# A row softmax on one core: tiles of twelve rows in four buffers instead of eight rows in six, with six of eleven stores moved to Pool's queue

## Chip, cores, metric

One core of a Trainium2 chip. The metric is the device time of one execution in microseconds (us), of which the span in a profile leaves out about 2. The kernel before takes 317.6 us.

## The reference

```python
"x": np.random.randn(32, 512, 1024).astype(np.float32), "temperature": 0.5
scaled = x / temperature
shifted = scaled - np.max(scaled, axis=-1, keepdims=True)
exp_x = np.exp(shifted)
return (exp_x / np.sum(exp_x, axis=-1, keepdims=True)).astype(np.float32)
```

There are 16,384 rows of 1,024 float32, so 128 rows of the matrix for each of the 128 partitions. 67.1 MB are read and 67.1 MB written.

## The kernel before

A tile holds `ROWS` consecutive matrix rows in each partition, so that each partition's part of a transfer is one contiguous piece (8 rows x 4 KB = 32 KB). It is loaded by SP, changed in place, and stored; its buffer then goes to a later load. A pass is a group of a tile's rows that goes through one maximum; `PASSES` lists the passes of each tile. VectorE (DVE) takes the maximum and divides by the sum, ScalarE (ACT) does the exponential with its sum. The code is abridged.

```python
ROWS = 8; BUFS = 6
PASSES = [[4, 4]] * 2 + [[8]] * 12 + [[4, 4]] * 2
WHOLE = (2, 4, 6, 8, 10, 12)     # tiles divided by one instruction
ALONE = 14
...
def maximum(g):
    nc.vector.tensor_reduce(out=top, in_=tiles[i][:, a:a+k, :], axis=X, op=extreme)
    nc.vector.tensor_scalar_mul(bias, in0=top, scalar1=-scale)
def exponential(g):
    for b in range(k):
        nc.scalar.activation(row, row, Exp, bias=bias[:, b:b+1], scale=scale, accum_out=sums[:, b:b+1])
def divide(g):
    nc.vector.reciprocal(recip, sums)
    if i in WHOLE: nc.vector.tensor_mul(xt, xt, recip.unsqueeze(2).to_broadcast([P, k, d]))
    else:          # row by row: tensor_scalar_mul
def store(g):      # g == 0: one row by Pool's queue; else, when the tile is done, by ACT's
    nc.scalar.dma_start(out=dram(of, i)[:, a:, :], in_=tiles[i][:, a:, :])
    load()         # the next tile, by SP's queue, when this store has landed
...
for g in range(len(groups) + 1):   # cut: the last tiles divide before the next maximum
    maximum(g); exponential(g); divide(g - 1); store(g - 1)
```

## Time and profile before

| | before |
|---|---|
| time, median | 317.61 us (317.17 to 317.79, 6 runs) |
| span of the profile | 315.7 us |
| DVE, ACT, Pool busy | 251.0, 148.1, 1.3 us |
| DMA, share of 16 engines | 99.0% |
| rate with loads and stores running | 433 GB/s |

On the page, a digit of the DMA row is the busy share of one fortieth of the span in tenths. q1 is SP's queue of loads, q10 ACT's queue, q0 Pool's. The lines themselves stand in the prediction.

### The profile page before, as it was taken

The page shows a single profiled execution, that of the slowest core. Times are in us where ns is not written, and L with a number is a line of the kernel's source. Part 1 is how long each engine was busy: PE and PEld are TensorE (multiplying, and loading weights), DVE is VectorE, ACT ScalarE, POOL GpSimd, SP SyncE. Part 2 cuts the span into 40 slices and gives each one's busy share as a digit, 9 for nine tenths or more (in the row PEclk, how much of TensorE's full clock was granted, in tenths as well). Part 3 has the DMA queues.
Part 4 walks back from the last instruction along what each step waited for, and adds up shares of the span by engine and source line. Part 5 has one row for each costly group of instructions (what it writes and reads, how often), then busy time and mean ns, then how long its engine had stood idle before and what let it go on. Part 6 is the DMA issues. An engine that isn't in the chain of part 4 may idle for free. (4 is left out here: it accounts for less than half of the span.)

```text
span 315.7 us, 534 instructions
## 1 busy us (share of the span) xinstructions
DVE 251.0 (79%) x146; ACT 148.1 (47%) x257; POOL 1.3 (0%) x5
## 2 busy tenths in 40 slices
DVE  0399999999679795897949979399793999979710
ACT  0176637680906519074290833808247091564700
POOL 0001000000000000000000000000000000000000
DMA  8999999999999999999999999999999999999996
GB/s 328 415 448 421 369 441 434 465 400 461 404 457 407 457 411 457 428 436 436 428 448 415 448 415 449 411 465 403 461 403 461 403 461 403 461 403 461 407 457 274
DMA packets 4755, 134.24 MB, mean 425 GB/s; under 512 B 528, under 2 KB 528, under 8 KB 656
## 3 DMA queue, kind: packets, MB, share of 16 engines
q1 hardware_dynamic: 2304, 67.11, 49.7%
q10 hardware_dynamic: 2304, 66.59, 48.9%
q0 software_dynamic: 144, 0.52, 0.4%
q14 instruction: 3, 0.02, 0.0%
HBM read 67.11 MB, written 67.11 MB: 425 GB/s over the span
## 5 line engine op out<-in xcount | busy, mean ns | idle before, releaser
L77 ACT ACTIVATE xt<-xt,bias 128x1024 f32<-128x1024 f32 x128 | 145.2, 1135 | 136.6 <-DVE bias L71 127.1
L68 DVE TENSOR_REDUCE top<-xt 128x8 f32<-128x8192 f32 (+1 forms) x20 | 139.5, 6976 | 44.4 <-DMA xt<-in_x_dram 44.4
L95 DVE TENSOR_SCALAR xt<-xt,recip 128x1024 f32<-128x1024 f32 x80 | 54.3, 748 | 0.5
L92 DVE TENSOR_TENSOR xt<-xt,recip 128x8192 f32<-128x8192 f32 x6 | 52.2, 8692 | 0.2
L77 ACT ACTIVATION_READ_ACCUMULATOR xt<-xt,bias 128x1 f32 x128 | 23.9, 187 | 0.0
L77 ACT ACT_TABLE_LOAD x1 | 1.3, 1283 | 13.3 <-DMA xt<-in_x_dram 13.3
L89 DVE RECIPROCAL recip<-sums 128x8 f32<-128x8 f32 (+1 forms) x20 | 3.8, 188 | 4.1 <-ACT xt L77 4.1
L71 DVE TENSOR_SCALAR bias<-top 128x8 f32<-128x8 f32 (+1 forms) x20 | 3.4, 171 | 0.7
L104 POOL DMA_DIRECT2D out_dram<-xt x1 | 1.1, 1142 | 23.4 <-DVE xt L95 23.4
L143 POOL MEMSET const-bfloat16-1.0<- 128x1 bf16 x1 | 0.1, 96 | 0.0
L143 POOL MEMSET const-float32-0.0<- 128x1 f32 x1 | 0.1, 93 | 0.2 <-issue 0.2
L143 POOL MEMSET const-float32-1.0<- 128x1 f32 x1 | 0.1, 93 | 0.0
L143 POOL MEMSET const-uint8-127<- 128x1 uint8 x1 | 0.1, 93 | 0.0
## 6 DMA issues: line engine op xcount, KB each, us to landing
xt<-in_x_dram SPq DMA_DIRECT2D x16, 4096.0 KB, 51.2
out_dram<-xt ACTq DMA_DIRECT2D x15, 4096.0 KB, 28.0
out_dram<-xt ACTq DMA_DIRECT2D x1, 3584.0 KB, 23.2
out_dram<-xt POOLq DMA_DIRECT2D x1, 512.0 KB, 19.6
```

The source lines that it names most:

```text
L68: nc.vector.tensor_reduce(out=top, in_=tiles[i][:, a : a + k, :], axis=mybir.AxisListType.X, op=extreme)
L71: nc.vector.tensor_scalar_mul(bias, in0=top, scalar1=-scale)
L77: nc.scalar.activation(tiles[i][:, a + b, :], tiles[i][:, a + b, :], mybir.ActivationFunctionType.Exp, bias=bias[:, b : b + 1], scale=scal ...
L89: nc.vector.reciprocal(recip, sums)
L92: nc.vector.tensor_mul(xt, xt, recip.unsqueeze(2).to_broadcast([P, k, d]))
L95: nc.vector.tensor_scalar_mul(tiles[i][:, a + b, :], in0=tiles[i][:, a + b, :], scalar1=recip[:, b : b + 1])
L104: nc.gpsimd.dma_start(out=dram(of, i)[:, :1, :], in_=tiles[i][:, :1, :])
L143: nc = _bacc.Bacc("TRN2", target_bir_lowering=False, num_devices=1)
```

## The change

The intent: larger pieces per partition (48 KB) at the same memory, passes of six rows, five of eleven tiles divided whole, and the first six stores taken out of ACT's instruction stream. The tiny copy ahead of the first store is there to hold it until the third load has landed. The diff is abridged.

```diff
-ROWS = 8
-BUFS = 6
+PASSES = [[4, 4, 4]] + [[6, 6]] * 9 + [[4, 4]]
+BUFS = 4
-PASSES = [[4, 4]] * 2 + [[8]] * 12 + [[4, 4]] * 2
-WHOLE = (2, 4, 6, 8, 10, 12)
+WHOLE = (2, 3, 4, 6, 8)
+BY_POOL = 6
-ALONE = 14
+ALONE = 9
 ...                       # cut: ROWS becomes rows[i] = sum(PASSES[i]) throughout
 def store(g):
-        if g == 0:
-            nc.gpsimd.dma_start(out=dram(of, i)[:, :1, :], in_=tiles[i][:, :1, :])
-        elif a + k == ROWS:
-            a = 1 if i == 0 else 0
-            nc.scalar.dma_start(out=dram(of, i)[:, a:, :], in_=tiles[i][:, a:, :])
+        if a + k == rows[i]:
+            if i == 0:
+                nc.gpsimd.tensor_copy(stats.tile([P, 1], f32, name="seen"), tiles[2][:, 0, 0:1])
+            queue = nc.gpsimd if i < BY_POOL else nc.scalar
+            queue.dma_start(out=dram(of, i), in_=tiles[i])
             load()
```

More of the change, by code (lines that the diff above doesn't have):

```diff
@@ L36 @@
     n, d = xf.shape
-    assert len(PASSES) * ROWS * P == n
+    rows = [sum(ks) for ks in PASSES]
+    assert sum(rows) * P == n
     data = ctx.enter_context(tc.tile_pool(name="data", bufs=BUFS))
@@ L44 @@
     for i, ks in enumerate(PASSES):
-        assert sum(ks) == ROWS
         for j, k in enumerate(ks):
@@ L49, in dram @@
     def dram(t, i):
-        block = t[P * ROWS * i : P * ROWS * (i + 1), :]
-        return block.rearrange("(p k) d -> p k d", p=P, k=ROWS)
+        block = t[P * sum(rows[:i]) : P * sum(rows[: i + 1]), :]
+        return block.rearrange("(p k) d -> p k d", p=P, k=rows[i])
     tiles, small = [], []
@@ L57, in load @@
         if i < len(PASSES):
-            xt = data.tile([P, ROWS, d], f32, name="xt")
+            xt = data.tile([P, rows[i], d], f32, name="xt")
             nc.sync.dma_start(out=xt, in_=dram(xf, i))
```

## The prediction

> **What bounds the kernel now.** I read first the page's slices of the span and its DMA rows, to see whether any resource is full.
>
> ```profile
> span 315.7 us, 534 instructions
> DVE 251.0 (79%) x146; ACT 148.1 (47%) x257; POOL 1.3 (0%) x5
> ...
> DMA  8999999999999999999999999999999999999996
> ...
> q1 hardware_dynamic: 2304, 67.11, 49.7%
> q10 hardware_dynamic: 2304, 66.59, 48.9%
> q0 software_dynamic: 144, 0.52, 0.4%
> ```
>
> The reader is to see that no compute engine is full, but the 16 DMA engines are at 9 tenths in every slice but the first and the last. Loads (q1, issued by SP) and stores (q10 by ACT, q0 by Pool) together fill 49.7 + 48.9 + 0.4 = 99.0% of 16 engines' span. Second, the busy time by stretches, to see the rate when both directions run and what is lost at the ends (columns: stretch, its length, DVE, ACT, POOL busy, clock, DMA share, GB/s).
>
> ```profile
> 1.50:15.70 14.20, 2.49 (x1) 1.28 (x1) 0.00 (x0) 1.00 0.99 406
> 15.70:29.00 13.30, 13.02 (x10) 9.16 (x16) 1.14 (x1) 1.00 1.01 435
> 29.00:60.00 31.00, 30.79 (x22) 18.44 (x32) 0.00 (x0) 1.00 1.01 422
> ...
> 137.40:260.00 122.60, 102.45 (x46) 61.41 (x109) 0.00 (x0) 1.00 1.00 433
> 260.00:300.97 40.97, 36.67 (x38) 20.17 (x36) 0.00 (x0) 1.00 1.00 432
> 300.97:313.20 12.23, 0.00 (x0) 0.00 (x0) 0.00 (x0) 1.00 0.99 429
> 313.20:315.70 2.50, 0.00 (x0) 0.00 (x0) 0.00 (x0) 1.00 0.03 13
> ```
>
> The plateau is 433 GB/s with the engines at 1.00. The last store is issued at 300.97, and the transfers stay full until 313.2: the tail is a backlog of stores being drained, not a wait for compute. So the chain that ended last (DVE and ACT, 6% each) names the last store's cause, but shortening it would only put the last store deeper into the backlog. Third, the waits of SP's own queue: is a load late because its buffer is not free?
>
> ```profile
> SPq L59 <- DMA out_dram<-xt: 214.3, 10, 42.9
> ```
>
> Ten loads do wait, for the store that frees their buffer. That is the way a full pipe looks, not a fault: the engines have no gap meanwhile.
>
> Last, durations. DVE's groups by shape:
>
> ```profile
> L68 DVE TENSOR_REDUCE top<-xt 128x8 f32<-128x8192 f32 x12 | 104.2, 8684 | 31.2 <-DMA xt<-in_x_dram 31.2
> L95 DVE TENSOR_SCALAR xt<-xt,recip 128x1024 f32<-128x1024 f32 x80 | 54.3, 748 | 0.5
> L92 DVE TENSOR_TENSOR xt<-xt,recip 128x8192 f32<-128x8192 f32 x6 | 52.2, 8692 | 0.2
> L68 DVE TENSOR_REDUCE top<-xt 128x4 f32<-128x4096 f32 x8 | 35.3, 4412 | 13.2 <-DMA xt<-in_x_dram 13.2
> ```
>
> A whole multiply costs 8692/8 = 1.09 us a row, the row-by-row one 54.3/80 = 0.68 us. DVE's waits are for loads: it follows the DMA.
>
> **The packets.** 2304 packets for 16 loads is 144 a load: 128 rows of 32 KB, one per partition, and 16 small ones that signal the end. The trace's packet records give 1.213 us for 32,768 bytes (median), 1.062 for 28,672 and 0.159 for Pool's 4,096. The slope between 4 and 32 KB is (1.213 - 0.159)/28,672 = 0.0000368 us a byte, or 27.2 GB/s an engine, and 8 ns a packet are left over. Per engine the kernel before moves 248 packets of 32 KB and, of the split first store, 8 of 28 KB and 8 of 4 KB: 248 x 1.213 + 8 x (1.062 + 0.159) = 310.6 us. First packet at 1.77 us, so 3.3 us are everything else: slow first packets (some 2 us instead of 1.2), engines that end 0.9 to 1.3 us after the rest, 1.2 us of closing.
>
> **What the Trainium skill says.** "DMA: Bandwidth & Descriptors", section "Where 436 GB/s comes from", gives a ceiling of 435.2 GB/s for the 16 ports; the plateau of 433 agrees and leaves 0.5% to win. "Issuing engines are not separate DMA queues" on that page says that issuing from several engines saves only issue time; the shares above agree that there is one pool of engines. The same page, "SWDGE vs HWDGE vs iDMA", says Pool's descriptors are made in software and that a packet is preferably at most 4096 bytes; before shows only one Pool store, with 4 KB rows, so no run yet shows what Pool does with 48 KB rows. "SBUF — State Buffer", section "Who interferes with whom", says a fp32 scalar multiply can lock Pool out of the port pair while the reduce never does and the two-tensor multiply holds only the read side; the 0.68 against 1.09 us a row fits two modes, but no wait of Pool here shows the lock.
>
> **The change, part by part.**
> (1) Tiles of 12 rows. 10 tiles of 12 and one of 8 replace 16 of 8. A 48 KB row, if it stays one packet, takes 0.159 + 45,056 x 0.0000368 = 1.815 us (an estimate). Per engine: 160 x 1.815 + 16 x 1.213 = 309.8 us against 310.6: a gain of 0.8 us, on the path, since the DMA is the path.
> (2) Four buffers: 4 x 48 KB = 6 x 32 KB, the same 192 KB a partition, 25.2 MB preloaded either way. Free to the total, but each buffer comes back in lumps of 6.3 MB.
> (3) Passes of six. DVE gets 18 reduces of 4.412 + 2 x 1.068 = 6.55 us and 5 of 4.41: 139.9 us (before 139.5). Whole multiplies 60 rows x 1.09 = 65.2 (before 52.2), row by row 68 x 0.68 = 46.2 (before 54.3), and three more pairs of small instructions at 0.36 us, 1.1 us. Sum +6.4, so DVE busy about 257. That lies beside DMA: a 12-row tile costs DVE at most 2 x (6.55 + 0.36 + 6.54) = 26.9 us when whole, 21.9 when not, while its load and store take 16 x 1.815 = 29.0 us. Spare: 2.1 us a tile at the least.
> (4) Stores 0 to 5 by Pool, behind a one-element copy that waits for the third tile's load. It holds store 0 from about 38 us (its last multiply) to about 47 us. In that time loads three and four still fill the engines, so nothing is lost. Pool's issue took 1.14 us before; six of them are 7 us on an idle engine. Each falls just behind the last multiply of its tile, when DVE begins a reduce of 6.5 us, which does not hold the ports. What it spares: ACT no longer carries these stores between its exponentials, but ACT idles 136.6 us, so nothing.
> (5) The end is like before: a last tile of 8 rows in passes of four.
>
> I then stepped the changed program order through with these durations, the rings served in turn packet by packet. The same bookkeeping ends the kernel before at 314.9 (measured span 315.7; loads land every 19.4 us, as in the trace). For the changed kernel it ends at 314.2, with no gap in the DMA. Closest place: about 74 us, where loads wait for store 0 to land (about 75.7) and only store 1 feeds the engines; it is issued near 69 us, some 4 us ahead. The difference is -0.7 us: 317.7 - 0.7 = **317.0 us**.
>
> **Rivals.**
> (a) Pool's rows are split in small packets. For: the skill's preference, and none of before's packets tells. Against: the skill's table in section "Bandwidth" has Pool's queue at 425 GB/s for 16 MB. If cut to 4 KB, 6 stores cost 576 packets x 0.159 = 91.6 us instead of 48 x 1.815 = 87.1, +4.5 us; and served in turn, loads would overtake the stores, so that compute, not backlog, sets the end: my stepping gives some +11 with 4 KB and +7 with 16 KB pieces, 324 to 328 us. I give this 7%.
> (b) Pool issues late, held by DVE or slow at making descriptors. For: the lock. Against: the reduce behind each issue. With 8 us lost per issue I get one gap of 2.4 us at 74 us, 319 to 320. 10%.
> (c) DVE becomes the bound because lumps are larger. If every tile were multiplied whole, the stepping shows gaps of 8 us in all (325); with five it shows none. Against it stands the 2.1 us spare. 5%.
> (d) Better ends: the late engines could catch up, worth at most 1.3 us; 315.7. Below that there is only the 309.8 us of packets plus 1.8 and 1.2 at the ends (312.8 of span, some 314.8 of time): over 2% faster, under 311.4, is ruled out by the bytes.
>
> **Range and chances.** The main line is 317.0 with about half a microsecond of doubt about the ends. Down I go to 315.8 for (d), up to 319.5 for a single gap of (b). Faster 0.01, same 0.92, slower (over 324.0) 0.07, nearly all of it (a).
>
> **What would show it.** Right: span near 315.0; DMA slices of 9 from the second on; plateau 433 to 434 GB/s; 144 packets a transfer on all queues, of 1.82 us; DVE near 257 us with waits only for loads; Pool's six issues of about 1.1 us each; the last store issued near 300 us with 12 us of backlog. Wrong: Pool's queue with more than 144 packets a store (a); a slice of 7 or less near 74 us, or Pool issues of several us (b); a last store issued after 303 us, or a slice under 9 before the end (c).

## The result

| | before | after |
|---|---|---|
| time, median of 6 | 317.61 us | 317.32 us (317.07 to 317.53) |
| ratio | | 0.9993, 95% interval 0.998 to 1.0006 |
| ratio, second chip job | | 0.9994 (0.9982 to 1.0005), medians 317.41 and 317.41 |
| span of the profile | 315.7 us | 315.8 us (315.4 in the second job) |

A ratio is the mean time of one kernel's runs over that of the other's in the same rounds, so it is not quite the ratio of the medians. Executions over 1.5% slower than the fastest of the same kernel are left out of the means. The two kernels take the same time. The prediction was 317.0, with 315.8 to 319.5 as its range.

First the page of the changed kernel.

```profile
span 315.8 us, 525 instructions
...
DVE 256.9 (81%) x147; ACT 148.3 (47%) x257; POOL 3.7 (1%) x11
...
DMA  8999999999999999999999999999999999999996
...
q1 hardware_dynamic: 1584, 67.11, 49.7%
q0 software_dynamic: 864, 37.75, 27.6%
q10 hardware_dynamic: 720, 29.36, 21.5%
```

The DMA row is the same as before, digit for digit. 1584 packets for 11 loads and 864 for Pool's 6 stores are 144 each: 128 rows and 16 signals. So a 48 KB row stayed one packet on every queue, Pool's too. The shares sum to 98.8%, 0.2 points under before. Next the busy time by stretches, with the columns as in the prediction.

```profile
29.00:46.00 17.00, 16.86 (x15) 9.09 (x17) 0.00 (x0) 1.00 0.97 422
46.00:60.00 14.00, 13.93 (x13) 11.32 (x21) 0.85 (x2) 1.00 1.03 414
...
137.40:176.00 38.60, 31.76 (x18) 14.94 (x27) 0.53 (x1) 1.00 1.01 435
176.00:260.00 84.00, 72.12 (x39) 40.93 (x72) 0.53 (x1) 1.00 1.00 433
```

The plateau is 433 to 435. The weak stretch is where the stores join the loads, from 48 us on, as a finer cut shows:

```profile
48.00:56.00 8.00, 7.93 (x6) 5.32 (x11) 0.56 (x1) 1.00 0.95 356
56.00:64.00 8.00, 8.00 (x5) 5.10 (x10) 0.00 (x0) 1.00 1.11 479
```

A packet counts where it starts, so part of the 356 comes back in the next stretch; what is really lost is worked out below. Last, SP's waits and the groups by shape.

```profile
SPq L60 <- DMA out_dram<-xt: 241.2, 7, 74.3
...
L69 DVE TENSOR_REDUCE top<-xt 128x6 f32<-128x6144 f32 x18 | 117.9, 6547 | 19.5 <-DMA xt<-in_x_dram 19.5
L93 DVE TENSOR_TENSOR xt<-xt,recip 128x6144 f32<-128x6144 f32 x10 | 65.6, 6558 | 0.4
L96 DVE TENSOR_SCALAR xt<-xt,recip 128x1024 f32<-128x1024 f32 x68 | 46.2, 749 | 0.5
...
L108 POOL DMA_DIRECT2D out_dram<-xt x6 | 3.3, 554 | 129.6 <-ACT xt L78 82.7
```

All seven later loads wait for a store, as ten did before. DVE's reduce of six rows takes 6.55 us and Pool's issue 0.55 us. DVE follows the loads, as before.

### Where the packets' gain went

The trace records each packet's start and duration. Two readings of these records answer the question.

**Distance from start to start.** Where loads and stores alternate, the first end-of-load signal of a load comes every 19.36 us before (86.90, 106.27, 125.63), which is 16 packets, so 1.2103 us for 32 KB. After, it comes every 29.00 us (137.58, 166.58, 195.58): 1.8125 us for 48 KB. The recorded durations are 1.213 and 1.815; a packet starts some 3 to 4 ns before the last one ends. With two further sizes from the experiments (4 KB: 0.1554, 16 KB: 0.6073) one line fits all four: 36.78 ps a byte plus 4.7 ns a packet. The prediction's 8 ns was the cost of packets laid end to end.

**Lost engine time.** For a stretch I take its length and subtract, for each packet, what it should take (8.4 ns + 36.76 ps a byte, the law of the durations), summed over the packets and divided by 16 engines. What is left is time in which the engines moved less than they could. In both kernels this is within 0.1 us of zero for every 8 us, but for the beginning, the place where the stores join, and the end:

```
us lost, mean of 16 engines       before (32 KB)     after (48 KB)
first packets (2 to 8 us)         0.70               0.87
stores join the loads             0.72 (32 to 40 us) 1.00 (48 to 56 us)
an engine's last packet ends      313.21 to 314.49   312.83 to 314.53
```

These repeat. In six profiles with 48 KB packets (the two of the changed kernel, e1, e2, e7, e10) the first is 0.86 to 0.95 and the second 0.93 to 1.09. In a second profile with 32 KB packets (b_whole_all) they are 0.68 and 0.72.

The second loss sits in load packets alone. In the changed kernel 20 of them, started between 49.6 and 54.4 us, take 1.90 to 3.31 us instead of 1.815; the first store packet starts at 52.26 us, and the store packets there take 1.81 as usual. What holds the loads up is not in the records.

The balance: 264 packets an engine become 176, so 88 x 4.7 ns = 0.41 us gained. 0.17 us are lost at the first packets and 0.28 us where stores join. That leaves +0.04 us, which is nothing.

### The profile page after: what moved, and what is told of

It reads as the page before. It is cut to its first block, busy times and chain, and to the rows that moved or that the text cites. A ratio compares the mean times of both kernels' runs of the same rounds, so it can differ in the third digit from the quotient of the medians.

```text
span 315.8 us, 525 instructions
## 1 busy us (share of the span) xinstructions
DVE 256.9 (81%) x147; ACT 148.3 (47%) x257; POOL 3.7 (1%) x11
## 3 DMA queue, kind: packets, MB, share of 16 engines
q1 hardware_dynamic: 1584, 67.11, 49.7%
## 4 chain that ended last, share of the span: by engine, by line
DMA 47%; DVE 28%; ACT 11%; issue 9%; DVEq 0%; SPq 0%; POOLq 0%
DMA xt<-in_x_dram 25%; DMA out_dram<-xt 22%; DVE top L69 16%; ACT xt L78 11%; DVE xt L96 8%; DVE xt L93 2%; DVE bias L72 0%; DVE recip L90 0%; DVEq L158 0%; SPq L60 0%; POOLq L108 0%
## 5 line engine op out<-in xcount | busy, mean ns | idle before, releaser
L69 DVE TENSOR_REDUCE top<-xt 128x6 f32<-128x6144 f32 (+1 forms) x23 | 139.9, 6083 | 37.8 <-DMA xt<-in_x_dram 37.8
L93 DVE TENSOR_TENSOR xt<-xt,recip 128x6144 f32<-128x6144 f32 x10 | 65.6, 6558 | 0.4
L96 DVE TENSOR_SCALAR xt<-xt,recip 128x1024 f32<-128x1024 f32 x68 | 46.2, 749 | 0.5
L90 DVE RECIPROCAL recip<-sums 128x6 f32<-128x6 f32 (+1 forms) x23 | 4.2, 182 | 5.0 <-ACT xt L78 5.0
L108 POOL DMA_DIRECT2D out_dram<-xt x6 | 3.3, 554 | 129.6 <-ACT xt L78 82.7
L72 DVE TENSOR_SCALAR bias<-top 128x6 f32<-128x6 f32 (+1 forms) x23 | 3.9, 171 | 0.8
```

The source lines that it names most:

```text
L69: nc.vector.tensor_reduce(out=top, in_=tiles[i][:, a : a + k, :], axis=mybir.AxisListType.X, op=extreme)
L96: nc.vector.tensor_scalar_mul(tiles[i][:, a + b, :], in0=tiles[i][:, a + b, :], scalar1=recip[:, b : b + 1])
L108: queue.dma_start(out=dram(of, i), in_=tiles[i])
```

## The experiments

All are edits of the changed kernel, except b_whole_all. Each is timed against the kernel before, on one chip for one job: e1 to e4 together; a_again, e8, e5, e6 together; e9, b_whole_all, e7 together; e10 alone.

### e3_pk4k: packets of 4 KB in place of 48

```diff
-return block.rearrange("(p k) d -> p k d", p=P, k=rows[i])
+return block.rearrange("(k p) d -> p k d", p=P, k=rows[i])
```

> The changed kernel with rows dealt to the partitions so that each packet is 4 KB instead of 48 KB, in both directions; tiles, passes, order and bytes are the same. Theory A2 (what counts is the distance from one packet's start to the next, 4.4 ns + bytes x 36.76 ps as fitted to the landings of both kernels, since each packet starts 4 ns before the last ends): 2048 packets an engine x 0.155 = 317.4 us against 309.3, so +8 us, less up to 1 us for smaller losses at the first packet and where stores begin: 324 to 325.5. The prediction's law (8.4 ns a packet, packets end to end): 2048 x 0.159 = 325.6 against 309.8, +15.8 us: 332 to 333. Rival (packet size is nothing): 317.3.

Measured: 325.97 us, ratio 1.0273 (1.0259 to 1.0286), so +8.7 us. The queues of its page:

```profile
q1 hardware_dynamic: 16560, 67.11, 50.8%
q0 software_dynamic: 9312, 37.75, 28.2%
q10 hardware_dynamic: 7248, 29.36, 22.0%
```

There are 33,120 packets instead of 3,168, and the shares sum to 101.0%, over 100: durations overlap. 2048 packets an engine x 0.1554 us = 318.3 against 176 packets' 309.4 is +8.9. The law of durations, which the prediction used, asked for +15.8. So packets cost what their starts say, and half of the prediction's gain was never there. The total is still 0.5 us above the 324 to 325.5 expected. One part of that: 4 KB loads alone, before any store, come 0.160 us apart, which is 1.2 us lost between 8 and 52 us. (Loads of 48 KB come 1.8125 apart with stores or without.)

### e9_pk16k: packets of 16 KB

```diff
-return block.rearrange("(p k) d -> p k d", p=P, k=rows[i])
+return block.rearrange("(h p k) d -> p h k d", p=P, h=rows[i] // 4, k=4)   # tile viewed alike
```

> The changed kernel with every row of 48 KB cut in packets of 16 KB (of the 32 KB rows of the last tile in two), both directions; all else alike. Theory A3 (two terms against each other: 4.4 ns a packet at each packet's start, and one loss of some 0.55 of a packet where stores first join the loads): 512 x 4.4 ns against 176 x 4.4 = +1.5 us, and a joining loss of some 0.35 us instead of 1.0, so +0.8 us, 318.0 to 318.4. The prediction's law with nothing against it (8.4 ns a packet): +2.8 us, 320.1. Rival (joining loss dominates, smaller packets are better): under 317.

Measured: 318.3 us, ratio 1.0041 (1.0025 to 1.0058), +1.3 us, within what A3 asked for and well under the prediction's law. Its two one-off losses are 0.49 us at the first packets (0.81 with 4 KB, so no simple rule in the size) and 0.72 us at the joining, not the 0.35 that I had scaled from the packet's size. Where loads and stores have like packets, the joining loss is under 0.2 us with 4 KB, 0.72 with 16 and with 32 KB, and 1.0 with 48: it grows with the packet, but not in proportion. Between 32 and 48 KB the two terms cancel.

### a_again and e8_first8k: can the loss at the joining be avoided?

a_again has no edit. e8's:

```diff
+            if i == 0:
+                for b in range(0, rows[0], 2):
+                    queue.dma_start(out=dram(of, 0)[:, b : b + 2, :], in_=tiles[0][:, b : b + 2, :])
+            else:
                 queue.dma_start(out=dram(of, i), in_=tiles[i])
```

> The changed kernel itself, in the same rounds as the next runs, so that differences of a few tenths can be read. Expected 0.998 to 1.001 of the kernel before; the accounts of lost engine time again 0.87 us at the first packets and 1.0 us where the first store meets the loads.

> The changed kernel with only its first store cut in six, of two rows each, so 8 KB packets instead of 48; everything else alike. So far the loss where stores join the loads was 0.03 us with 4 KB packets, 0.72 with 32 KB and 1.00 with 48 KB. Theory M (the loss is paid once, by the first stores, in proportion to their packets): about 0.2 us instead of 1.0, the 48 packets an engine cost 0.16 us more, so 0.6 to 0.7 us faster than the changed kernel in the same rounds. Rival (the loss waits for the first large store packet): no loss at store 0 but 0.7 to 1.0 us when store 1 begins, and the total is 0.1 to 0.2 us slower.

Measured: a_again 317.41 us, 0.9994, with losses of 0.89 and 1.00. e8 319.37 us (318.08 to 321.48), 1.0058. The total is 2.0 us above a_again's, where 0.6 less (M) or 0.2 more (the rival) had been expected. Theory M falls: 0.16 us are lost from 48 to 56 us, where store 0 joins with its 8 KB packets, but another 0.76 us between 60 and 64. The rival falls too. It put the second loss at the first large store packets; they start at 76.08 us, and from 64 to 80 us nothing is lost, nor more than 0.03 us from 80 to 88, where loads run beside them.

```profile
60.00:64.00 4.00, 4.00 (x1) 1.38 (x4) 0.00 (x0) 1.00 0.96 328
64.00:68.00 4.00, 3.93 (x7) 2.58 (x5) 0.00 (x0) 1.00 1.00 424
```

The time goes in the last 16 packets of the fourth load, one per engine: they take 2.42 to 2.77 us instead of 1.815, while the stores beside them are still of 8 KB. The small packets let that load past the store: it lands at 65.0 instead of 72.8 us. e6 below, with 4 KB stores beside 48 KB loads, shows the same: 0.13 us from 48 to 56, 0.87 from 56 to 64, in the last packets of the fourth load. So with small stores nearly the whole loss is still paid, later, by the loads, and large store packets are not needed for it. A further 0.51 us are lost between 128 and 136 us, again in load packets (24 of them, up to 2.39 us): an engine runs out of stores at 128.68 us, and store 3's first packet starts at 130.54. What the engines do in these microseconds the trace doesn't tell, and how to avoid the loss stays open.

### e6_pool4k: rival (a) by itself

Pool's stores go to permuted rows (the edit is abridged: the store then writes to `to`), so that their packets are 4 KB beside loads of 48 KB. The result is wrong in order on purpose.

```diff
+            if i < BY_POOL:
+                to = (rows of tile i).rearrange("(k p) d -> p k d", p=P, k=rows[i])
```

> The changed kernel with Pool's six stores in 4 KB packets beside loads of 48 KB: the rows go to other places of the output on purpose, so the result is wrong in order, with the same bytes. The prediction's rival a by itself. If rings take turns packet by packet, loads overtake stores by 12 to 1 in bytes, the loads end early, and the end hangs on compute: stepping gives +23 us, about 340, with the gap late (290 us on). If turns go by bytes, only the packets' cost remains: 48 x (12 x 0.155 - 1.81) = +2.3 us, about 319.6.

Measured: 331.9 us (330.3 to 334.1), ratio 1.0468, +14.9 us: between the two figures, with the first one's mechanism. From 50 to 62 us, where store 0 and the fourth load run together, the DMA queues of that stretch read:

```profile
q1 hardware_dynamic: 85, 4.18, 88.5%
q0 software_dynamic: 64, 0.26, 5.3%
```

Turns go by packet, not by bytes: 21 of the 85 loads start before the first store packet, at 53.38 us, and from there it is 64 to 64, a load's turn carrying twelve times a store's. The fourth load lands at 63.8 us instead of 72.8. The hole comes later, at 230 to 260 us. Pool's stores have fallen behind: store 5, issued at 172.76, lands at 244.2, and SP holds the next load, which needs its buffer, from 199.6 to 244.63:

```profile
180.00:230.00 50.00, 29.98 (x14) 19.92 (x36) 0.00 (x0) 1.00 1.00 417
230.00:260.00 30.00, 25.30 (x15) 13.80 (x24) 0.00 (x0) 1.00 0.87 347
```

So rival (a) would have been worse than feared (+11 said for 4 KB, here +15). It did not happen because Pool keeps 48 KB rows whole.

### e5_pool_late: rival (b)

The edit also makes a pool of one buffer for the scratch (cut here).

```diff
+            if i < BY_POOL:
+                late = lates.tile([P, 2048], f32, name="late")
+                nc.gpsimd.tensor_copy(late[:, 0:1], tiles[i][:, rows[i] - 1, 0:1])
+                for _ in range(4):
+                    nc.gpsimd.memset(late, 0.0)
             queue.dma_start(out=dram(of, i), in_=tiles[i])
```

> The changed kernel with four fills of an 8 KB-per-partition scratch by Pool ahead of each of its six stores, after the multiply that the store waits for; the delay is read from the trace (I expect 7 to 9 us in all). The prediction's rival b by itself. My stepping: 4 us late costs 0.4 us, 6 to 8 us cost 2.4 us in one gap near 74 us, 10 us 4.5, 12 us 5.7. Rival (a late store is made up later, for the engines have a backlog): no change within 0.3 us.

Measured: 321.86 us and, for the profiled run, 322.89, ratio of these runs 1.0152, so +4.8 us. Two other runs took 334.3 and 334.6, and I did not find out what they are. Around store 1 (start, duration):

```profile
70.52 0.18 POOL L111 COPY late<-xt 128x1 f32<-128x1 f32 x1 [14.18 <-issue]
...
70.76 7.39 POOL L113 MEMSET late<- 128x2048 f32 x4
...
76.89 1.28 DVE L73 TENSOR_SCALAR bias<-top 128x6 f32<-128x6 f32 x1
...
77.13 0.33 SPq L61 DMA_DIRECT2D xt<-in_x_dram  x1
...
78.09 0.53 POOL L114 DMA_DIRECT2D out_dram<-xt  x1
```

Store 1 is issued at 78.09 instead of 69.47, 8.6 us late. The engines lose 2.57 us between 72 and 80, about the 2.4 stepped. They lose 1.49 us more between 80 and 100, in load packets of up to 3.44 us where the loads start again, and some 0.4 after; the stepping had neither. The prediction's closest place, near 74 us, is real; its cost for 8 us was half of the measured one. The edit isn't rival (b) alone, though: the fills hold DVE too. At each of the six stores DVE's small multiply takes 1.2 to 1.4 us instead of 0.17 and ends 0.02 to 0.03 us after the last fill. What share of the 4.8 us that has was not tested. In the changed kernel Pool is never late: each issue takes about 0.55 us and follows its multiply within half a microsecond or so.

### e4_whole_all and b_whole_all: rival (c), and what the buffers do

```diff
-WHOLE = (2, 3, 4, 6, 8)
+WHOLE = tuple(range(11))     # b_whole_all: the kernel before with range(16)
```

> The changed kernel with all eleven tiles multiplied whole. My stepping says DVE then takes 26.9 us of the 29.0 that a tile's transfers take, but the early stores and the end come late: gaps of some 2.4 us near 74 us, 2 us near 106 us and 4 us near 306 us, so +8 us, 325 to 326. Rival (DVE has slack in every tile and the total stays with the bytes): 317.3. A second rival (DVE is already the bound and 68 rows x 0.41 us come on top in full): +28 us, 345.

> The kernel before (six buffers of eight rows) with all sixteen tiles multiplied whole, as in e4 with eleven, where it cost the four-buffer kernel 11 us. Theory (large lumps cost tolerance: a buffer that comes back every 29 us leaves a deeper hole when its store is late than one every 19 us): stepping says +0.5 us, 317.5 to 319. Rival (it is only DVE's sum, +28 to 33 us of busy time in both kernels, and buffers have nothing to do with it): +10 us or more, like e4.

Measured: e4 328.63 us (four runs, 328.1 to 332.4), ratio 1.0382 (1.0341 to 1.0423), so +11 to +12 us. b_whole_all 317.85 us, 1.0016 (1.0003 to 1.0029). DVE is busy for 285.0 us in e4 and 283.5 us in b_whole_all, the same load. First e4, then b_whole_all, around the place where the third part of the buffers comes back:

```profile
72.00:80.00 8.00, 7.93 (x5) 6.90 (x12) 0.03 (x1) 1.00 0.78 296
80.00:100.00 20.00, 19.79 (x8) 7.32 (x13) 0.50 (x1) 1.00 0.97 388
```

```profile
72.00:80.00 8.00, 8.00 (x2) 4.36 (x8) 0.00 (x0) 1.00 1.05 455
80.00:100.00 20.00, 19.93 (x5) 9.16 (x16) 0.00 (x0) 1.00 0.98 423
```

In e4 the second store is issued at 79.97 instead of 69.47 and the engines run dry, as in e5; more is lost in the end (2.6 us between 280 and 300, 1.0 between 310 and 313). With six buffers of eight rows the same DVE load costs half a microsecond. The two kernels differ in buffers, rows a tile, passes and store queues at once, so which of these took the slack is not separated. The change paid nothing in time for its lumps, but it gave up slack, and its choice of five whole tiles (none of the first two, none of the last two) is what keeps it clear of the hole.

### e2_no_hold: without the held copy

```diff
-                nc.gpsimd.tensor_copy(stats.tile([P, 1], f32, name="seen"), tiles[2][:, 0, 0:1])
```

> The changed kernel without the one-element copy that holds store 0 until the third tile has landed, so store 0 is issued near 38 us instead of 47.9. Theory A: the engines are full in either order, so the total is the same within 0.3 us; the loss where the first store meets the loads (1.0 us in the changed kernel between 48 and 56 us) moves to some 38 us and keeps its size. Rival: the hold avoids an early gap (near 70 us, when loads wait for buffers) and without it the kernel is 1 us or more slower.

Measured: 317.69 us, ratio 1.0024 (0.9997 to 1.005), with single runs from 316.9 to 320.36: the same at 2%, and too scattered to tell tenths. The trace tells more: store 0 is issued at 47.82 us instead of 47.89. The third pass of tile 0 is multiplied only from 44.8 to 47.4 us; the copy held nothing. The loss at the joining stayed at 48 to 56 us (0.93), so my 38 us was wrong and the question whether an earlier store 0 would matter was not put.

### e1_all_act, e7_all_pool, e10_all_act_again: who issues

```diff
-BY_POOL = 6
+BY_POOL = 0      # e1 and e10, and without the copy; e7: BY_POOL = 11, with it
```

> The changed kernel with all eleven stores by ACT's queue and without the one-element copy. Theory A (the DMA engines are the bound and who issues is free): within 0.3 us of the changed kernel, so about 317.3, no slice of the DMA row under 9 after the first. Rival B (Pool's queue is what ate the packets' gain, by descriptors made in software): 0.5 to 0.8 us faster, about 316.6. Rival C (ACT's order holds back stores, which is why the change moved them): slower by 1 us or more, with gaps in the DMA.

> The changed kernel with all eleven stores by Pool's queue instead of six. Theory A (who issues is free): within 0.3 us of the changed kernel, 0.998 to 1.001 of the kernel before. Rival (Pool's late stores are held behind row-by-row multiplies, and the last one ends later): 1 us or more slower, with the last store's landing later than 314.5.

> The same kernel as e1 (all stores by ACT's queue, no held copy) once more, because one store queue measured 1.0014 (ACT) and 1.0020 (Pool) of the kernel before while the split of six and five measured 0.9993 and 0.9994. If the split does help by some 0.5 us, this gives 1.001 to 1.002 again, with the last DMA engine ending after 314.6 while the first ends near 312.9. If it was the scatter of the chip or of the rounds, this gives 0.9985 to 1.0005.

Measured, against the kernel before in the same rounds:

```
                         median   ratio (95%)                first engine ends   last
e1  all by ACT           317.72   1.0014 (1.0003 to 1.0026)  312.82              314.97
e10 all by ACT again     318.57   1.0029 (1.0013 to 1.0045)  312.91              315.86
e7  all by Pool          318.05   1.0020 (1.0008 to 1.0032)  312.93              314.80
after, 6 by Pool         317.32   0.9993 (0.998 to 1.0006)   312.83              314.53
a_again                  317.41   0.9994 (0.9982 to 1.0005)  312.91              314.13
e2, 6 by Pool, no copy   317.69   1.0024 (0.9997 to 1.005)   312.99              314.76
```

None of the expectations is met in full. Pool's queue does not eat the gain (rival B of e1), and no gap comes (rival C): the mean engine time lost up to 313 us is 3.5 to 3.7 us in all six. One store queue is 0.4 to 0.9 us slower than the kernel before by these ratios, three times out of three, and the split twice level with it. That looks like a gain of 0.6 to 1.1 us for two queues, but it is a difference between jobs on different chips. The one pair in the same rounds says otherwise: e2 (two queues, without the copy that held nothing anyway) has a median of 317.69, e1 (one queue) 317.72. So a gain from two queues is not shown. What differs in the profiles is how far the 16 engines drift apart: the first ends alike, the last between 314.13 and 315.86, with e2 near e7. Why is not shown.

No version beat both kernels, and no experiment pointed to one: packets of 4, 16, 32 and 48 KB were tried, and the best two are those of the two kernels, which tie.

## Why the prediction was right, and where its steps were off

**The bound.** Right. The DMA row did not change by a digit, SP's loads still wait for stores, and DVE's extra 5.9 us (251.0 to 256.9; 257 had been said) did not show. The DMA stays full until the last store has drained: it is issued at 301.35 us, over 11 us before the first engine ends.

**Part 1, the packets.** The mechanism was right and the size off. The duration, 1.815 us, was met to the nanosecond, and on Pool's queue too. The term that failed is the sum "160 x 1.815 + 16 x 1.213 = 309.8 us against 310.6": it laid packets end to end, while they start 3 to 4 ns early. With the measured distance the gain is 0.41 us instead of 0.8 (e3 and e9 confirm the distance). And "3.3 us are everything else" was taken as fixed, while two of its parts were larger with 48 KB than with 32 KB, by 0.17 and 0.28 us. By this account the -0.7 us should have been nothing; measured are -0.07% and -0.06% of 317, about -0.2 us and inside the noise. That the number came within 0.3 us of 317.32 is in part luck: the terms that failed come to 0.8 us.

**Part 2, four buffers.** Right for the time, but not free: e4 against b_whole_all, 11 us against half a microsecond for the same DVE load, shows slack that was given up.

**Part 3, passes of six.** Right: 6.547 us a reduce (6.55 said), no DVE wait for anything but loads and ACT's sums.

**Part 4, Pool.** Half wrong. The copy holds store 0 for 0.1 us, not 9: "about 38 us (its last multiply)" was the second of three passes. The issue cost 0.55 us rather than 1.1. That moving the stores spares nothing is not contradicted: in the same rounds two queues (e2, 317.69) and one (e1, 317.72) are alike.

**The rivals.** (a) is real as a mechanism (e6, +15 us, turns by packet) and did not occur. (b) is real (e5): the place was right, the cost for 8 us, 2.4, measured 4.8, with DVE held as well. (c) is real (e4): +8 said, +11 measured. None occurred, because the kernel's choices keep clear of each. (d) did not come either.

## What to carry to other kernels

When the transfers fill the DMA engines, first work out the floor in packets, from start to start and not from durations; here pieces of 32 and 48 KB tie as the best of the four sizes tried, and the rest is a few fixed microseconds. A change that leaves the time alone can still spend slack: larger lumps in fewer buffers are fine until a store is late. And keep the packets of queues that share engines alike in size, since turns go by packet.

## What the Trainium skill lacked or had wrong

- "DMA: Bandwidth & Descriptors", section "SWDGE vs HWDGE vs iDMA", prefers packets of at most 4096 bytes for Pool's queue. Here Pool's stores are recorded as 128 packets of 48 KB at 1.815 us, the same as on the other queues, and 4 KB packets on all queues cost 8.7 us in 317 (e3).
- The same page, section "Queues, rings and completion order", says that engines take turns between queues at packet granularity. The runs agree, but the page does not say what follows when packets differ: turn by turn, 64 load packets of 48 KB went beside 64 store packets of 4 KB, and the kernel lost 15 us (e6).
- The same page, section "Issuing engines are not separate DMA queues", says that issuing from several engines saves only issue time. The runs do not show it wrong: one queue for all stores measured 1.0014, 1.0029 (ACT) and 1.0020 (Pool), two queues 0.9993, 0.9994 and 1.0024, and in the same rounds one and two were alike (317.72 and 317.69).
- No page has the one-off loss where stores join running loads: 0.72 us with 32 KB packets, 1.0 us with 48 KB, all of it in load packets; nor by how much a packet starts before the last one ends, some 3 to 4 ns here.
- "SBUF — State Buffer", section "Who interferes with whom", warns of DVE holding up Pool's descriptors. No run here shows it: Pool's issues took 0.53 to 0.67 us each, and each fell in a DVE reduce, where the page expects none. e5 shows only the reverse, DVE held by Pool's fills for over 1 us at each of six stores.
